# A transformer trunk on one core: a third chunk of the down projection by seven products, one weight sum by an adding transfer, and a buffer pair moved by some hundred bytes

## The chip, the cores and the metric

The kernel runs on one core of one Trainium2 chip. The metric is the device time of one execution in microseconds. The engines of a core are TensorE (PE, with its weight loads shown as PEld), VectorE (DVE), ScalarE (ACT), GpSimd (POOL) and SyncE (SP, which here only issues transfers). About 0.2%, 4.6 us, is what a measurement of this kernel can tell from no change.

## The reference

A two-layer encoder over 256 positions of width 2048, in float32:

```
h = x
h = h + mixer_a(rms_norm(h), ...)      # grouped-query attention, 16 heads
h = h + conv_ffn(rms_norm(h), ...)     # layer 0
h = h + mixer_b(rms_norm(h), ...)      # three dilated groups, 24 heads
h = h + conv_ffn(rms_norm(h), ...)     # layer 1
return rms_norm(h)

conv_ffn: u = conv3(h @ w_up) + b;  gate, val = split(u);  (silu(gate) * val) @ w_down
```

`w_up` is 2048 x 11264 and `w_down` is 5632 x 2048 in each layer. The change lies in the product with `w_down`.

## The kernel before

**Precision by splitting.** The kernel multiplies in a rounded form of float32 (type fp32r). Each operand is therefore cut into a high part (a rounding copy on ACT) and a low part (the rest, a subtraction on DVE), and a product takes three matmuls: high x high, low x high, high x low. For the weights, `split_raw` (line 116 on) makes `wh` (ACT, line 119) and `wl` (DVE, line 120) of each 128 x 1024 block. The activations, once split, are kept in `ah`/`al` tiles ("forms", 128 x 256 each).

**The buffers of the weights.** Six raw buffers `raw0` to `raw5` (`new_raw`) take blocks of 512 KB from memory, all issued from SP in program order. The ring `hl_ring` holds three pairs `wh`/`wl`. For the down projection a fourth pair, tag 9, is put in front of the ring (line 611) and taken out after it (line 657). The split of unit i can start when PE has used the pair of unit i-4.

**The FFN.** `ffn` (line 405) goes in two halves: `HALVES` gives 6 and then 5 pairs of 512-row chunks of the inner dimension. Each half first computes its part of the up projection (`feed_T`), the convolution (`up_post`) and the gate product (`glu` or `glu_forms`, the product on POOL), and then adds its part of the down projection to `h`. So the down projection's chunks are numbered 0 to 5 in a first half and 0 to 4 in a second.

**Seven products for eight.** In `project_pair` (line 214) the down projection works on two 512-column blocks of the output at once. A chunk is a 2 x 2 block problem: two blocks of 128 positions, 512 rows of weight as two 256-row blocks, two column blocks. A plain chunk takes 4 units of kind "c" with 12 matmuls each. A chunk listed in `SKG` is done by the Strassen-Winograd scheme: 7 units of kind "P" with 6 matmuls each. It needs sums of weight blocks (`prepare`, line 236: 11 += 12 for product 5, 12 += 22 for product 7, 22 += 11 for product 6, 21 += 22 for product 4; each is one DVE addition over 128 x 1024, line 241) and sums of activations (`glu_forms`). The four raw blocks 11, 12, 21, 22 of such a chunk are held until their last product, so two raw buffers are left for the plain units between. A first half runs two such passes (columns 0 and 1, then 2 and 3); a second half one, and the two other columns plainly (`project`).

**PSUM.** The pass uses all eight banks: M1, M5, M6, M7 for products that are combined afterwards, and C11, C21, C12, C22, to which plain units and the products 2, 3 and 4 add directly. `combine` (line 616) and `done` (line 555) bring them into `h` on DVE; they run a step at a time after units.

**The order of units** (lines 603 to 609): one plain unit, then each product followed by one plain unit, then the rest. `ORDER` gives the order of the products within a chunk. `late_at` marks the first unit of the last chunk, before which all pending work on the activations is drained.

**Priority.** Tile schedules instructions by program order; `tc.high_priority(offset=AHEAD)` lets a split or a weight sum go as if it had been written 45 instructions earlier. Each engine then works through its own list strictly in order.

**Where the tiles lie.** Pools are stacked in the order they are opened. In the program before, the forms of the outer pool (24 pairs), the inputs of the up projection and the three pairs `wh0` to `wl2` all start 448 bytes past a multiple of 1 KB in each partition. The FFN's own pool starts 704 bytes past one. In it lie, among others, the last six forms of a first half and the fourth pair:

| | FFN 0 | FFN 1 |
|---|---|---|
| `wh9`, bytes past a multiple of 1 KB | 768 | 768 |
| `wl9` | 896 | 768 |
| forms 24 to 29 | 896 | 768 |

In FFN 0 `bias_lines` (line 885) borrows the fourth pair's tiles during the up projection, to write position-bias lines for mixer B to memory.

Of the kernel before, what the change touches and what calls it, by code (L numbers as in the profile page):

```python
# [20 lines left out]
HALVES = ((0, 6), (6, 11))  # L21
SCALE = 128.0 ** -0.5
NRAW, NHL = 6, 3
SKG = ((0, 2), (0,))
ORDER = (1, 2, 5, 3, 7, 6, 4)
AHEAD = 45
NWARM = 11

# [2 lines left out]
def tile_encoder(ctx: ExitStack, tc: tile.TileContext, x, xT, w_a, w_ao, q_gain, k_gain, w_b, w_bo,  # L31
# [25 lines left out]
    def nm(s):  # L57
        uid[0] += 1
        return f"{s}_{uid[0]}"
# [154 lines left out]
    def project_pair(w, n0, n1, lhs, forms, units, late, early_done, n0_done):  # L214
        home = {1: "M1", 2: "C11", 3: "C12", 4: "C21", 5: "M5", 6: "M6", 7: "M7"}
        place = ("M1", "M5", "M6", "M7", "C11", "C21", "C12", "C22")
        b = bank_at[0]
        acc = {k: bank((4, 5, 6, 7, 2 - b, 3 - b, b, b + 1)[i], "acc") for i, k in enumerate(place)}

        def touched(u):  # L220
            return (home[u[2]],) if u[0] == "P" else (("C11", "C21"), ("C12", "C22"))[u[2] // 2]

        first, last = {}, {}
        for i, u in enumerate(units):
            for k in touched(u):
                first.setdefault(k, i)
                last[k] = i
        blocks = {}
        sums = {5: ("11", "12"), 7: ("12", "22"), 6: ("22", "11"), 4: ("21", "22")}

        def block(kg, b):
            if (kg, b) not in blocks:
                blocks[kg, b] = load_raw(w, (n0, n1)[int(b[1]) - 1], kg, int(b[0]) - 1)
            return blocks[kg, b]

        def prepare(u):
            kind, kg, p = u
            if kind == "P" and p in sums:
                dst, src = (block(kg, b) for b in sums[p])
                with tc.high_priority(offset=AHEAD):  # L240
                    nc.vector.tensor_tensor(dst, dst, src, ALU.add)
                if p == 6:
                    done_raw(blocks.pop((kg, "11")))
                elif p == 4:
                    done_raw(blocks.pop((kg, "22")))

        last_s = max(i for i, u in enumerate(units) if u[0] == "P")
        for i, (kind, kg, p) in enumerate(units):
            if i == late:
                drain()  # L250
            if kind == "c":
                r = load_raw(w, (n0, n1)[p // 2], kg, p % 2)
            else:
                b = {1: "11", 2: "21", 3: "22", 5: "11", 7: "12", 6: "22", 4: "21"}[p]
                r = block(kg, b)
            if i + 1 < len(units):
                prepare(units[i + 1])
            wh, wl = split_raw(r, kind == "c" or p in (7, 4))
            if kind == "P" and p in (7, 4):
                blocks.pop((kg, b))  # L260
            todo = []
            if kind == "c":
                for j in range(2):
                    for m, k in enumerate(touched((kind, kg, p))):
                        todo.append((k, *at(lhs[4 * kg + 2 * (p % 2) + j], m), j))
            else:
                xh, xl = forms[kg][p]
                for j in range(2):
                    todo.append((home[p], xh[:, j * P:(j + 1) * P], xl[:, j * P:(j + 1) * P], j))
            fresh = {k for k in acc if first[k] == i}  # L270
            for k, xh, xl, j in todo:
                nc.tensor.matmul(acc[k], xh, wh[:, j, :], start=k in fresh, stop=False)  # L272
                fresh.discard(k)
                nc.tensor.matmul(acc[k], xl, wh[:, j, :], start=False, stop=False)  # L274
            todo.sort(key=lambda t: (t[0], t[3]))
            for k, xh, xl, j in todo:
                nc.tensor.matmul(acc[k], xh, wl[:, j, :], start=False, stop=last[k] == i and j == 1)  # L277
            if i == last_s:
                early_done(acc)
            if i == last["C21"]:  # L280
                n0_done(acc)
            step()
        return acc
# [119 lines left out]
        more()  # L403

    def ffn(l, hT, ss_in, g_next, last, side=None):
        with tc.tile_pool(name=nm("fpool"), bufs=1) as fp:
            junk = junk_of(fp)
            rstd = finish_rstd(ss_in)
            part = small.tile([P, 2], F32, tag="part", name=nm("part"), bufs=1)
# [3 lines left out]
            rows = conv[l].rearrange("b o (r c) -> (b o r) c", c=P)  # L413
            nc.gpsimd.dma_start(cr[:, 0:2, :], rows[0:2 * P].rearrange("(a p) c -> p a c", p=P))
            nc.gpsimd.dma_start(cr[:NROW - 2 * P, 2, :], rows[2 * P:NROW])
            cw = fp.tile([P, NROW], F32, name=nm("cw"))

            def taps():
                t = ps_tile()
# [87 lines left out]
            kgs = list(range(4))  # L507
            for hf, (p0, p1) in enumerate(HALVES):
                slots, forms = {}, {}
                tags = iter([(hpool, k) for k in range(24)] + [(fp, k) for k in range(24, 30)])  # L510

                def new_form():
                    pool, k = next(tags)
# [2 lines left out]
                for p in range(p0, p1):  # L516
                    if p - p0 in SKG[hf]:
                        fm = forms[p - p0] = {f: new_form() for f in (1, 7, 2, 5, 4, 6, 3) + (0,) * hf}
                        if hf:
                            for kt in range(4):  # L520
                                slots[4 * (p - p0) + kt] = [
                                    tuple(t[:, kt % 2 * P:(kt % 2 + 1) * P] for t in fm[f])
                                    for f in ((1, 0), (2, 4))[kt // 2]]
                    else:
                        slots.update({4 * (p - p0) + j: new_form() for j in range(4)})
                    for hh in range(2):
                        cg = fp.tile([P, 2, NT], F32, tag="cg", name=nm("cg"), bufs=2)
                        cv = fp.tile([P, 2, NT], F32, tag="cv", name=nm("cv"), bufs=2)

                        def after(cg=cg, cv=cv, slots=slots, forms=forms, kg=p - p0, hh=hh):  # L530
                            if kg in forms:
                                return glu_forms(cg, cv, forms[kg], hh)
                            return glu(cg, cv, slots, 4 * kg + 2 * hh)

                        ga, va = new_acc(), new_acc()
                        parts = ([0, 1], [2], [3]) if p == 0 and hh == 0 else ([0, 1], [2, 3])
                        if len(parts) == 3:
                            for k, kk in enumerate(parts):
                                if k == 2:
                                    drain()  # L540
                                feed_T(ga, hT, w_up[l], p, hh, kk, k == 0, k == 2)
                                if k == 2:
                                    start(up_post(ga, p, hh, cg))
                                feed_T(va, hT, w_up[l], NPAIR + p, hh, kk, k == 0, k == 2)
                        else:
                            for k, kk in enumerate(parts):
                                feed_T(ga, hT, w_up[l], p, hh, kk, k == 0, k == 1)
                            start(up_post(ga, p, hh, cg))
                            for k, kk in enumerate(parts):
                                feed_T(va, hT, w_up[l], NPAIR + p, hh, kk, k == 0, k == 1)  # L550
                        start(up_post(va, NPAIR + p, hh, cv, after))
                    if p == 1 and side is not None:
                        spare.append(side(fp))

                def done(accs, n):
                    if hf == 1 and last:
# [45 lines left out]
                        fin.append(f)  # L602
                cs = [("c", k, i) for k in range(np_) if k not in SKG[hf] for i in range(4)]
                ps = [("P", k, p) for k in SKG[hf] for p in ORDER]
                per = max((len(cs) - 4) // len(ps), 1)
                units = [cs.pop(0)]
                for u in ps:
                    units += [u] + [cs.pop(0) for _ in range(per)]
                units += cs
                late_at = next(i for i, u in enumerate(units) if u[1] == np_ - 1)  # L610
                hl_ring.insert(0, (fp, 9))

                def hcol(m, n):
                    return h[:, m, n * 512:(n + 1) * 512]
# [38 lines left out]
                else:  # L653
                    seq = [k for k in range(np_)]
                    for n in (2, 3):
                        done(project(wd, n, slots, seq, last and hf == 1 and n == 3), n)
                hl_ring.remove((fp, 9))
            assert not spare
        return hTn, ss

# [221 lines left out]
    scr0 = dpool.tile([8, P, 512], F32, name="scr0")  # L882
    scr1 = dpool.tile([16, P, 256], F32, name="scr1")

    def bias_lines(lp):
        if True:
            oh = lp.tile([P, 1024], F32, tag="wh9", name="oh")
            nc.gpsimd.dma_start(oh, onehot)
            rb = lp.tile([P, 32], F32, name="rb")[:, :24]
            nc.gpsimd.memset(rb, 0.0)  # L890
            nc.gpsimd.memset(rb[32:33, :], -1e30)
            nc.gpsimd.dma_start(rb[:32, :], rel_bias)
            lh = lp.tile([P, 24, 32], F32, tag="wl9", name="lh")
            nc.vector.tensor_copy(lh, rb[:, :, None].to_broadcast([P, 24, 32]))
            for b in range(6):
                for _ in range(2):
# [2 lines left out]
                t = ps_tile()  # L899
                nc.tensor.matmul(t[:, :w], lh[:, 4 * b:4 * b + 4, :].rearrange("p a r -> p (a r)"),  # L900
                                 oh[:, c0:c0 + w], start=True, stop=True)
                ln = lp.tile([P, 512], F32, tag="ln", name=nm("ln"), bufs=2)
                nc.vector.tensor_copy(ln[:, :w], t[:, :w])
                dst = scr0[4 * b:4 * b + 4] if b < 2 else scr1[4 * (b - 2):4 * (b - 2) + 4]
                for i in range(4):
# [223 lines left out]
```

## Time and profile before

| | us |
|---|---|
| median of three runs | 2300.05 |
| lowest, highest run | 2299.35, 2300.75 |
| the profiled execution | 2300.93 |
| its span in the trace | 2299.2 |
| first half's down projection, FFN 0 | 543.6 to 670.2 |
| second half's, FFN 0 | 893.7 to 1001.9 |
| first half's, FFN 1 | 1831.4 to 1958.3 |
| second half's, FFN 1 | 2181.8 to 2290.2 |

The profile's page gives the busy time of each engine, the chain of waits that ended last (followed back from the last instruction), and the costliest groups of instructions: line, engine, operation, output <- inputs, shapes, count | busy us, mean ns of one | idle time of the engine before them and what ended it. A matmul's mean is from its start to its end; matmuls are pipelined. Rows of windows give, for a stretch of time, its length and each engine's busy time with the count of instructions, the granted clock, the DMA engines' busy share and GB/s. Rows of waits give who waited for whom: us in total, times, longest. Rows of transfers end with the median us from issue to landing.

### The profile page before, as it was taken

How to read it: one execution, taken by the hardware profiler on the slowest of the kernel's cores; microseconds unless marked ns; L12 is line 12 of the kernel's file. 1: busy time of each engine (PE TensorE's matmuls, PEld its weight loads, DVE VectorE, ACT ScalarE, POOL GpSimd, SP SyncE). 2: the span in 40 equal slices, each digit the busy share in tenths (PEclk: the TensorE clock that was granted, in tenths of full speed). 3: DMA queues.
4: the chain of work that ended last, by engine and by line, in shares of the span. 5: the costliest groups of instructions: out<-in, count | busy, mean ns of one | idle time of the engine just before them, and what ended most of it. 6: DMA issues, size and time to landing. Idle time of an engine off the chain costs nothing.

```text
span 2299.2 us, 31196 instructions
## 1 busy us (share of the span) xinstructions
PE 2281.6 (99%) x11581; PEld 1935.0 (84%) x11581; DVE 1732.5 (75%) x2483; ACT 1248.6 (54%) x1802; POOL 168.5 (7%) x130
## 2 busy tenths in 40 slices
PE   9999999999999999999999999999999999999998
PEld 7788788888888888888888888878888888888886
DVE  6877887777877778878876876576777788777774
ACT  6565565555545556445454454445555555565553
POOL 2210000010001010010000000000101000001110
PEclk9999999999999999999999999999999999999999
DMA  8444565765666555666655555566565566565663
GB/s 300 154 141 156 189 197 175 245 202 186 207 196 191 186 184 181 207 215 202 190 176 178 178 188 168 176 190 192 189 192 187 173 217 202 184 191 185 202 211 128
DMA packets 260313, 437.54 MB, mean 190 GB/s; under 512 B 13904, under 2 KB 196944, under 8 KB 260160
## 3 DMA queue, kind: packets, MB, share of 16 engines
q1 hardware_dynamic: 258080, 429.84, 58.3%
q0 software_dynamic: 1648, 5.15, 0.8%
q8 instruction: 90, 1.47, 0.3%
q14 instruction: 63, 0.52, 0.1%
q10 hardware_dynamic: 432, 0.56, 0.1%
HBM read 429.20 MB, written 6.29 MB: 189 GB/s over the span
## 4 chain that ended last, share of the span: by engine, by line
PE 93%; DVE 3%; DMA 1%; issue 1%; POOL 1%; ACT 0%; SPq 0%; POOLq 0%; DVEq 0%; ACTq 0%
PE acc L143 28%; PE acc L146 14%; PE acc L165 11%; PE acc L166 11%; PE acc L164 11%; PE acc L272 5%; PE acc L274 5%; PE acc L277 5%; DVE wl L120 1%; DVE tT L333 1%; PE ps L304 1%; DMA raw<-in_w_up_dram 1%; PE ps L308 1%; PE ps L307 1%; PE ps L306 0%
## 5 line engine op out<-in xcount | busy, mean ns | idle before, releaser
L119 ACT ACTIVATE wh<-raw 128x1024 fp32r<-128x1024 f32 x822 | 866.4, 1059 | 780.0 <-PE acc L166 276.5
L120 DVE TENSOR_TENSOR wl<-raw,wh 128x1024 fp32r<-128x1024 f32 x822 | 1007.7, 1231 | 369.5 <-ACT wh L119 356.8
L143 PE MATMUL acc<-xh,wh 128*128 128x512 f32 x2816 | 707.2, 393 | 0.8 <-ACT wh L119 0.8
L143 PEld LDWEIGHTS acc<-xh,wh 128*128 128x128 f32 x2816 | 507.0, 189 | 93.2 <-ACT wh L119 1.6
L146 PEld LDWEIGHTS acc<-xh,wl 128*128 128x128 f32 x2816 | 384.1, 190 | 27.5
L146 PE MATMUL acc<-xh,wl 128*128 128x256 f32 x2816 | 392.6, 282 | 0.0
L165 PE MATMUL acc<-wl,xh 128*128 128x512 f32 x768 | 300.2, 391 | 3.5 <-DVE wl L120 2.1
L164 PE MATMUL acc<-wh,xh 128*128 128x512 f32 x768 | 301.8, 394 | 0.0
L166 PE MATMUL acc<-wh,xh 128*128 128x512 f32 x768 | 299.5, 390 | 0.0
L272 PE MATMUL acc<-wh,ah 128*128 128x512 f32 x524 | 205.7, 393 | 0.0
L274 PE MATMUL acc<-wh,al 128*128 128x512 f32 x524 | 205.2, 392 | 0.0
L165 PE MATMUL acc<-wl,ah 128*128 128x512 f32 x480 | 188.0, 392 | 2.0 <-DVE wl L120 1.8
L164 PE MATMUL acc<-wh,ah 128*128 128x512 f32 x480 | 187.8, 391 | 0.0
L166 PE MATMUL acc<-wh,al 128*128 128x512 f32 x480 | 187.3, 390 | 0.0
L165 PEld LDWEIGHTS acc<-wl,xh 128*128 128x128 f32 x768 | 144.4, 188 | 34.0 <-DVE wl L120 4.6
L166 PEld LDWEIGHTS acc<-wh,xh 128*128 128x128 f32 x768 | 144.2, 188 | 30.0
L164 PEld LDWEIGHTS acc<-wh,xh 128*128 128x128 f32 x768 | 144.4, 188 | 27.8
L277 PE MATMUL acc<-wl,ah 128*128 128x512 f32 x524 | 146.9, 391 | 0.0
L466 POOL TENSOR_TENSOR cv<-cg,cv 128x512 f32<-128x512 f32 x32 | 73.2, 2288 | 651.6 <-DVE cv L458 591.2
L272 PEld LDWEIGHTS acc<-wh,ah 128*128 128x128 f32 x524 | 98.4, 188 | 22.0 <-ACT wh L119 0.2
L277 PEld LDWEIGHTS acc<-wl,ah 128*128 128x128 f32 x524 | 98.4, 188 | 21.8
L274 PEld LDWEIGHTS acc<-wh,al 128*128 128x128 f32 x524 | 98.4, 188 | 21.6
(175 smaller groups left out, 1838.9 us busy)
## 6 DMA issues: line engine op xcount, KB each, us to landing
raw<-in_w_up_dram SPq DMA_DIRECT2D x352, 512.0 KB, 5.0
raw<-in_w_down_dram SPq DMA_DIRECT2D x176, 512.0 KB, 4.4
raw<-in_w_b_dram SPq DMA_DIRECT2D x144, 512.0 KB, 4.2
raw<-in_w_bo_dram SPq DMA_DIRECT2D x48, 512.0 KB, 3.7
raw<-in_w_a_dram SPq DMA_DIRECT2D x40, 512.0 KB, 3.7
raw<-in_w_ao_dram SPq DMA_DIRECT2D x32, 512.0 KB, 3.6
raw<-in_w_a_dram SPq DMA_DIRECT2D x16, 256.0 KB, 6.5
h<-in_x_dram SPq DMA_DIRECT2D x4, 512.0 KB
```

Of the source, the lines that this page charges most:

```text
L119: nc.scalar.activation(wh, r, AF.Copy)
L120: nc.vector.tensor_tensor(wl, r, wh.bitcast(F32), ALU.subtract)
L143: nc.tensor.matmul(acc[j], wh[:, kt, j * P:(j + 1) * P], lhs[4 * kg + kt][2], start=first and i == 0 and kt == 0, stop=False)
L146: nc.tensor.matmul(acc[j][:, :NT], wl[:, kt, j * P:(j + 1) * P], lhs[4 * kg + kt][0], start=False, stop=end and kt == 3)
L164: nc.tensor.matmul(accs[m], xh, wh[:, j, :], start=st, stop=False)
L165: nc.tensor.matmul(accs[m], xh, wl[:, j, :], start=False, stop=False)
L166: nc.tensor.matmul(accs[m], xl, wh[:, j, :], start=False, stop=sp)
L272: nc.tensor.matmul(acc[k], xh, wh[:, j, :], start=k in fresh, stop=False)
L274: nc.tensor.matmul(acc[k], xl, wh[:, j, :], start=False, stop=False)
L277: nc.tensor.matmul(acc[k], xh, wl[:, j, :], start=False, stop=last[k] == i and j == 1)
L304: nc.tensor.matmul(o, lh[ls], rh[rs], start=start, stop=stop)
L466: nc.gpsimd.tensor_tensor(cv, cg, cv, ALU.mult)
```

## The change

1. `SKG` of a first half becomes (0, 2, 4): a third chunk by seven products. The units between products are spread anew: a first half has 21 products and 12 plain units, so that plain units follow the 3rd, 5th, 7th, ... 21st product. A second half keeps one plain unit after each product. The products' order becomes 1, 2, 3, 5, 7, 6, 4.
2. The sum 11 += 12 for product 5 is no longer a DVE addition. After block 11 has been split for product 1, a transfer issued from GpSimd adds block 12 to it (SBUF to SBUF, 512 KB).
3. A new pool `wpool` is opened before the FFN's pool. It holds the taps `cw`, padded from 1408 to 1792 bytes, the forms 24 to 32, and the fourth pair. All but `cw` then lie at 704 + 1792 = 2496 = 2 x 1024 + 448 bytes, or a multiple of 1 KB further.
4. To make room, `bias_lines` takes its two line buffers as the halves of one tile that shares the place of a transposition buffer.

```diff
-SKG = ((0, 2), (0,))
-ORDER = (1, 2, 5, 3, 7, 6, 4)
+SKG = ((0, 2, 4), (0,))
+ORDER = (1, 2, 3, 5, 7, 6, 4)
...
-            if kind == "P" and p in sums:
+            if kind == "P" and p in sums and p != 5:
...
+            if kind == "P" and p == 1:
+                with tc.high_priority(offset=AHEAD):
+                    nc.gpsimd.dma_start(r, block(kg, "12"), accum_op=ALU.add)
...
-        with tc.tile_pool(name=nm("fpool"), bufs=1) as fp:
+        with tc.tile_pool(name=nm("wpool"), bufs=1) as wp, tc.tile_pool(name=nm("fpool"), bufs=1) as fp:
+            cw = wp.tile([P, 448], F32, name=nm("cw"))[:, :NROW]
...
-            cw = fp.tile([P, NROW], F32, name=nm("cw"))
...
-                tags = iter([(hpool, k) for k in range(24)] + [(fp, k) for k in range(24, 30)])
+                tags = iter([(hpool, k) for k in range(24)] + [(wp, k) for k in range(24, 33)])
...
-                per = max((len(cs) - 4) // len(ps), 1)
+                between = min(len(cs) - 2 - 6 * hf, len(ps))
                 units = [cs.pop(0)]
-                for u in ps:
-                    units += [u] + [cs.pop(0) for _ in range(per)]
+                for i, u in enumerate(ps):
+                    units.append(u)
+                    if (i + 1) * between // len(ps) > i * between // len(ps):
+                        units.append(cs.pop(0))
...
-                hl_ring.insert(0, (fp, 9))
+                hl_ring.insert(0, (wp, 9))
...
-    def bias_lines(lp):
+    def bias_lines(wp, lp):
...
+            lnt = lp.tile([P, 2, 512], F32, tag="tT", name="lnt")
...
-                ln = lp.tile([P, 512], F32, tag="ln", name=nm("ln"), bufs=2)
+                ln = lnt[:, b % 2]
```

More of the change, by code (lines that the diff above doesn't have):

```diff
@@ L552, in ffn @@
                     if p == 1 and side is not None:
-                        spare.append(side(fp))
+                        spare.append(side(wp, fp))
                 def done(accs, n):
@@ L656, in ffn @@
                         done(project(wd, n, slots, seq, last and hf == 1 and n == 3), n)
-                hl_ring.remove((fp, 9))
+                hl_ring.remove((wp, 9))
             assert not spare
@@ L883, in tile_encoder @@
     scr1 = dpool.tile([16, P, 256], F32, name="scr1")
-    def bias_lines(lp):
+    def bias_lines(wp, lp):
         if True:
-            oh = lp.tile([P, 1024], F32, tag="wh9", name="oh")
+            oh = wp.tile([P, 1024], F32, tag="wh9", name="oh")
             nc.gpsimd.dma_start(oh, onehot)
@@ L892, in bias_lines @@
             nc.gpsimd.dma_start(rb[:32, :], rel_bias)
-            lh = lp.tile([P, 24, 32], F32, tag="wl9", name="lh")
+            lh = wp.tile([P, 24, 32], F32, tag="wl9", name="lh")
+            lnt = lp.tile([P, 2, 512], F32, tag="tT", name="lnt")
             nc.vector.tensor_copy(lh, rb[:, :, None].to_broadcast([P, 24, 32]))
```

## The prediction

> **What bounds the kernel now.** I read the page's busy shares first, then the chain of waits, then the costliest groups.
>
> ```profile
> PE 2281.6 (99%) x11581; PEld 1935.0 (84%) x11581; DVE 1732.5 (75%) x2483; ACT 1248.6 (54%) x1802; POOL 168.5 (7%) x130
> ...
> PE 93%; DVE 3%; DMA 1%; issue 1%; POOL 1%; ACT 0%; SPq 0%; POOLq 0%; DVEq 0%; ACTq 0%
> ...
> L272 PE MATMUL acc<-wh,ah 128*128 128x512 f32 x524 | 205.7, 393 | 0.0
> ```
>
> PE is busy 99% and is 93% of the chain that ended last, so a matmul taken away shortens the end, as long as the other engines still feed PE. The trap is its price. The 393 ns of L272 is the time from a matmul's start to its end, and matmuls overlap. What one costs is the distance between starts, which the windows give: stretches of PE alone, with the count of weight loads (one for each matmul).
>
> ```profile
> 210.06:239.98 29.92, 29.92 (x133) 24.77 (x132) 26.20 (x42) 16.00 (x24) 0.00 (x0) 1.00 0.55 176
> ...
> 543.60:670.22 126.62, 103.69 (x553) 1.00 0.62 199
> 893.66:1001.90 108.24, 89.01 (x475) 1.00 0.60 195
> 1831.38:1958.32 126.94, 103.66 (x553) 1.00 0.62 199
> 2181.79:2290.20 108.41, 88.75 (x474) 1.00 0.49 160
> ```
>
> The first row lies in mixer A's output projection, which has no fourth pair: 132 matmuls in 29.92 us, 226.7 ns each. The other four rows (columns: length, PEld busy and count, clock, DMA share, GB/s) are the down projections, first and second half of FFN 0, then of FFN 1. By the code a first half has 552 matmuls (two passes of 14 units of 6 and 16 of 12) and a second half 474 (234 in the pair, 240 after it); one load at an edge is a neighbour's. At 226.7 ns these are 125.12 and 107.44 us. The stretches are longer by 1.50, 0.80, 1.82 and 0.97 us, 5.1 together. The starts of units say where, in the timeline of PE (start, length of one, line):
>
> ```profile
> 547.81 0.39 PE L272 MATMUL acc<-wh,ah 128*128 128x512 f32 x1
> ...
> 550.53 0.39 PE L272 MATMUL acc<-wh,ah 128*128 128x512 f32 x1
> ...
> 551.89 0.40 PE L272 MATMUL acc<-wh,ah 128*128 128x512 f32 x1
> ...
> 554.67 0.40 PE L272 MATMUL acc<-wh,ah 128*128 128x512 f32 x1
> ...
> 556.05 0.39 PE L272 MATMUL acc<-wh,ah 128*128 128x512 f32 x1
> ```
>
> These are the first matmuls of units 2 to 6. A plain unit of 12 takes 2.72 us, a product of 6 takes 1.36: 226.7 ns again. Unit 4, every fourth, is fed by the fourth pair, and takes 2.78; the next takes 1.38. Nobody waits there. By the program's addresses the three pairs of the ring and the 24 forms of the outer pool all lie 448 bytes past a multiple of 1 KB; the fourth pair lies at 768 and 896 (FFN 0) or 768 and 768 (FFN 1), and so do the last six forms.
>
> **Part one: a third chunk by seven products.** In one pass over two column blocks a plain chunk is 4 units of 12 matmuls, a chunk by products 7 of 6: 42 for 48. One chunk, two passes, two layers: 24 matmuls fewer, at 226.7 ns **5.4 us** less on the path.
>
> The page "TensorE: Matmul & The Clock Gate" of the Trainium skill, section "Back-to-back issue gap", gives about 131 ns for a sustained matmul of N=512. By that the part would be worth an estimated 3.1 us; the 132 matmuls above disagree, so I stay with 226.7.
>
> The price is more splits (ACT copy, DVE subtraction) for less PE time. DVE's timeline and its window over the second pass show how near it is:
>
> ```profile
> 586.59 1.22 DVE L120 TENSOR_TENSOR wl<-raw,wh 128x1024 fp32r<-128x1024 f32 x1
> 587.73 1.22 DVE L241 TENSOR_TENSOR raw<-raw,raw 128x1024 f32<-128x1024 f32 x1
> 588.86 3.49 DVE L120 TENSOR_TENSOR wl<-raw,wh 128x1024 fp32r<-128x1024 f32 x3
> ...
> 607.00:670.20 63.20, 63.20 (x277) 51.79 (x276) 51.38 (x51) 31.21 (x31) 0.00 (x0) 1.00 0.63 200
> ...
> L387 DVE TENSOR_TENSOR h<-acc,h 128x512 f32<-128x512 f32 x7 | 4.7, 684 | 0.7 <-PE acc L277 0.7
> ...
> ACT wh L119 <- PE acc L274: 44.1, 42, 3.1
> ...
> DVE raw L241 <- DMA raw<-in_w_down_dram: 8.0, 5, 3.2
> ```
>
> Back to back, splits and sums start 1.14 us apart. A pass before needs 30 splits and 8 sums, 43.3 us, and 12 operations of L387's kind (combination and residual) at 0.68, 8.2: 51.5, as the window's 51.38 shows, of 63.2. After: 33 splits and 9 sums (a tenth to twelfth go to the transfer), 47.9 + 8.2 = 56 us, of 21 x 1.36 + 12 x 2.72 = 61.2. So 92%, still under PE; with every sum on DVE it would be 59.5. Locally, P P c needs 3 splits and about 1 sum, 4.6 us of 5.4, and the tightest stretch, P5 P7 c P6 P4 c, 6 splits and 3 sums, 10.3 of 10.9: no debt, but no lead won either. ACT (33 copies of 1.06, 35 us) is far away. The lead is what hides all this. In the waits between 543 and 680 us ACT stands 44.1 us for PE to release a buffer: splits run at the ring's full depth. I cost the denser units at 0, hidden by that lead. Without it each of the 8 tight stretches (chunks 0 and 4, two passes, two layers) would make PE wait for about one DVE operation more: 8 x 1.14 = 9 us, the upper bound.
>
> Smaller things. The product P3 now makes C12 needed three units into a pass instead of four longer ones: in the second pass 5.44 us after its start. The two L387 additions that must clear C12 and C22 were done 3 us after the start (606.98):
>
> ```profile
> 608.73 1.28 DVE L387 TENSOR_TENSOR h<-acc,h 128x512 f32<-128x512 f32 x2
> ...
> L290 DVE TENSOR_TENSOR al<-st,ah 128x256 fp32r<-128x256 f32 x24 | 9.6, 419 | 0.0
> L289 ACT ACTIVATE ah<-st 128x256 fp32r<-128x256 f32 x24 | 9.5, 406 | 0.0
> ...
> 407.00:541.00 134.00, 133.24 (x761) 116.89 (x760) 102.85 (x154) 79.28 (x119) 13.18 (x6) 1.00 0.69 221
> ```
>
> That leaves 2.4 us: 0, at most 1 per layer if DVE has no lead then. And the third chunk's forms cost, once a layer, 3 more ACT copies (0.41), 3 more subtractions and 4 sums on DVE (0.42 each, 2.9 us), in the up stage, where DVE works 102.85 of 134: 0. The bias lines now alternate between halves of one tile; their six steps spread over 63 us, so 0.
>
> **Part two: the fourth pair's position.** The new pool starts where the old one did, 704 past a multiple of 1 KB, and its first tile is padded to 1792 bytes, so pair and late forms come to 448 like the others. If position is the cause, all of the 5.1 us go, except 0.1 that is a wait for a copy: **5.0 us**. Bounds: 0 (no effect) and 5.1.
>
> **Part three: the first sum by a transfer.** Off DVE, one sum per chunk and pass (14 in all). On POOL, 14 issues, each waiting for P1's subtraction and block 12. Behind it on POOL stands at most the last gate product, used only by the last chunk. On ACT and DVE P5's copy waits for the landing, and *every* later split stands behind that. No row shows an adding transfer; the nearest are POOL's plain ones:
>
> ```profile
> oh<-in_onehot_dram POOLq DMA_DIRECT2D x1, 512.0 KB, 5.1
> rb<-in_rel_bias_dram POOLq DMA_DIRECT2D x1, 3.0 KB, 4.6
> fin<-in_final_norm_dram POOLq DMA_DIRECT2D x4, 256.0 KB, 6.3
> ...
> DMA to landing us min/median/max: 6.1/6.3/7.1
> ...
> q1 hardware_dynamic: 258080, 429.84, 58.3%
> ```
>
> Lower bound 5.1 us, the plain 512 KB. The adding one must also read its destination: 429.84 MB in 58.3% of 2299.2 us is 321 GB/s, so one more pass over 0.524 MB is 1.6 us: 6.7. Upper bound: the slowest landing of POOL's queue (fin's, 7.1) and two passes more, 10.4. I take 6.7, since only the pass is new to the 512 KB row.
>
> The page "Collectives: The Full Stack", section "Part 3: Why 7× under link rate — side-by-side accounting", says that an add in a DMA costs no arithmetic but needs two source reads, which halves the rate. That speaks against the transfer as the row does; by a full doubling at the row's rate an estimate is the same 6.7.
>
> How long it may take: in chunks 0 and 2 P5 starts 6.8 us after P1 (three products and a plain unit between, P1 included), and its copy takes 1.1. With no lead at P1 the transfer may take 5.7; with the ring full (three units and a third, 5.9, less the split's 2.4) 3.5 more, 9.2. In chunk 4, with two plain units between, 8.4 to 11.9; in second halves still more. At 6.7 it costs something only where the lead is under 1.0 us. **I allow +1.0 us** in all. The load of weights grows to 206 GB/s and the transfers add 26 to 51, a share of 0.72 to 0.80 where it is 0.62 now: landings stay hidden as DVE's 8.0 us of waits for them are now.
>
> **The sum.** The profiled execution took 2300.93 us (span 2299.2, 1.7 around it), 0.9 above the median 2300.05. 2300.93 - 5.4 - 5.0 + 1.0 = 2291.5, against the median **2290.6**.
>
> **Rivals.**
> - *Only the count pays.* Position is not the cause and the slow units stay: 2300.05 - 5.4 + 1 = 2295.6. Against it: units of the three aligned pairs are at 226.7 to the nanosecond, and no wait stands there.
> - *DVE becomes the bound in the dense stretches.* 92% on average with no lead regained between P5 and P4; the 9 us of the upper bound above: 2300.05 - 10.4 + 9 = 2298.7. Against it: 5.2 us of slack per pass.
> - *The transfer lands late* (the other side). Place: the copy for P5, with all splits behind it. At the upper 10.4 us and the middle of 5.7 and 9.2, it is 2.9 us late in the 8 near chunks, and late by nearly nothing in the 4 far ones; ACT and DVE have to refill the lead in a stretch that gives none. 8 x 2.9 = 23 us, so 2300.05 - 10.4 + 23 = 2313. It becomes slower than before once the loss is over 10.4 us, that is 1.3 per near chunk: a transfer over 8.8 us. For it: all 16 engines are shared with loads at a share of 0.62, and the adding form is unknown. Against it: 512 KB on the same queue took 5.1.
>
> **How the numbers follow.** Forecast with 0 to 3 us of stalls (2288.5 to 2293): 0.60. Count alone: 0.08. DVE-bound or slightly late, 2293 to 2301: 0.12. Late transfer: 0.20. The range goes from 2288.5 (everything hidden, less the runs' spread) to 2303, leaving out most of the late transfer; the likeliest case's own range is 2288.5 to 2293. About 0.2% (4.6 us) can be told from no change: faster (under 2295.4) takes the forecast, half of the count alone and half of the third case, 0.70; the same 0.11; slower 0.19.
>
> **What would show it.** Matmuls of line 272 fall from 524 to 516. Every unit of the pairs takes 2.72 or 1.36 us, and the first halves 122.4 us each (540 matmuls). The transfers' landing is under 8 us and PE waits for ACT's copy less than 1 us in all. I am wrong if the fourth unit still takes 2.78, or if PE's idle before L272 is several us released by ACT, which itself waited for the transfer on P5.

## The result, and the profile after

| | us | ratio to before, 95% interval |
|---|---|---|
| before, median of the runs beside it | 2300.23 | |
| after, median of four runs (2315.5 to 2321.4) | 2317.3 | 1.0077 [1.0060, 1.0095] |
| predicted | 2290.6 (2288.5 to 2303) | |
| the profiled execution of after, its span | 2318.56, 2316.7 | |

The change makes the kernel 17 us slower. The page of the kernel after (busy shares, the chain of waits, two groups, one row of transfers):

```profile
PE 2284.1 (99%) x11557; PEld 1934.2 (83%) x11557; DVE 1747.4 (75%) x2511; ACT 1261.1 (54%) x1820; POOL 180.3 (8%) x144
...
PE 86%; DVE 6%; DMA 4%; issue 2%; ACT 1%; POOL 1%; SPq 0%; POOLq 0%; DVEq 0%; ACTq 0%
...
L275 PE MATMUL acc<-wh,ah 128*128 128x512 f32 x516 | 204.3, 396 | 1.9 <-ACT wh L119 1.9
...
L280 PE MATMUL acc<-wl,ah 128*128 128x512 f32 x516 | 149.6, 397 | 15.0 <-DVE wl L120 14.9
...
raw<-raw POOLq DMA_DIRECT2D x14, 512.0 KB, 6.8
```

The 24 matmuls are gone (516 for 524 on each of three lines), yet PE is busy longer and has fallen from 93% to 86% of the chain; DVE and DMA have taken the difference. PE now stands 14.9 us ahead of line 280, the matmuls with the *low* part of the weights, which DVE makes. The wait that the prediction feared, before the high part (line 275, released by ACT), is only 1.9. The transfer lands in 6.8 us in the median; 6.7 was estimated. Its fastest and slowest landings stand in the view of the tile:

```profile
DMA to landing us min/median/max: 4.6/6.8/8.1
```

Where it happens, by windows over the four down projections (length, PE and PEld busy with counts, DVE, ACT, POOL, granted clock, DMA share, GB/s):

```profile
542.72:680.10 137.38, 128.22 (x542) 102.94 (x541) 111.33 (x113) 70.59 (x74) 6.45 (x6) 0.98 0.66 202
903.54:1011.80 108.26, 108.26 (x480) 89.64 (x479) 91.72 (x130) 54.55 (x74) 3.24 (x1) 1.00 0.60 195
1840.39:1974.62 134.23, 128.11 (x542) 102.96 (x541) 111.30 (x113) 70.72 (x74) 6.41 (x6) 0.97 0.67 206
2198.06:2306.50 108.44, 106.88 (x470) 87.54 (x469) 66.50 (x70) 47.64 (x59) 13.24 (x7) 1.00 0.51 164
```

A first half should take 540 x 0.2267 = 122.4 us. It takes 137.4 and 134.2: 15.0 and 11.8 us lost. By the starts of its units, the pair pass of FFN 1's second half loses 2.5 more, that of FFN 0's nothing. So some 29 us are lost against 10.4 gained; the span is 17.5 us longer, so that the 1.4 us between lie outside the down projections. The waits say to what:

```profile
DVE raw L241 <- DMA raw<-raw: 40.2, 12, 5.4
...
PEld acc L280 <- DVE wl L120: 22.6, 19, 3.4
...
PE acc L280 <- DVE wl L120: 14.9, 13, 3.0
...
ACT wh L119 <- DMA raw<-raw: 10.4, 7, 2.0
```

DVE's *sums* (line 241) stand 40.2 us for the adding transfer, 12 times, up to 5.4. ACT's copies, where the prediction put the wait, stand 10.4. PE's longest stall, in chunk 4 of FFN 0's first pass, in the chain of waits (start, length, what):

```profile
583.68 8.10 DMA raw<-raw
...
591.88 1.06 ACT wh L119
592.95 1.23 DVE wl L120
594.18 0.04 issue
594.22 0.80 PE acc L280 x2
```

and the same moments in the timelines of DVE, ACT and PE:

```profile
591.80 1.23 DVE L241 TENSOR_TENSOR raw<-raw,raw 128x1024 f32<-128x1024 f32 x1 [4.32 <-DMA raw<-raw]
592.95 2.36 DVE L120 TENSOR_TENSOR wl<-raw,wh 128x1024 fp32r<-128x1024 f32 x2
...
587.06 1.06 ACT L119 ACTIVATE wh<-raw 128x1024 fp32r<-128x1024 f32 x1 [0.83 <-DMA raw<-in_w_down_dram]
...
590.18 0.39 PE L275 MATMUL acc<-wh,ah 128*128 128x512 f32 x1
```

Which blocks these are, the program's instruction list for DVE tells (in its order: line, output <- inputs):

```
L241 raw_5653<-raw_5653,raw_5692    12 += 22, for product 7; waits for the transfer
L120 wl_5695<-raw_5692,wh_5694      low part for product 3
L120 wl_5707<-raw_5704,wh_5706      low part of the plain unit
L241 raw_5692<-raw_5692,raw_5647    22 += 11, for product 6
L120 wl_5724<-raw_5647,wh_5723      low part for product 5
```

The sum 12 += 22 overwrites block 12, which the transfer reads. So it waits for the landing, and in DVE's list it stands *ahead of product 3's subtraction*. Product 3's copy was done at 588.12 (587.06 + 1.06), its subtraction could have run then, and it ran at 592.95. PE, which began product 3 at 590.18 and needs the low part at its fifth matmul, stood until 594.22. Product 5's copy, at 591.88, was in time: by the units' lengths PE would have come to it at 590.18 + 1.36 + 2.72 = 594.26.

In FFN 1's second half the same sum waits 4.98 us, against 2.34 in FFN 0's, which loses nothing:

```profile
2201.86 1.23 DVE L241 TENSOR_TENSOR raw<-raw,raw 128x1024 f32<-128x1024 f32 x1 [4.98 <-DMA raw<-raw]
```

Behind it in DVE's list stand, beside splits, the last steps of the convolution. They come later there, and with them the gate product and the copy of its form, ahead of a weight copy on ACT that PE then waits for. That this is the whole 2.5 us is read from one trace and was not tested.

### The profile page after: what moved, and what is told of

Read it like the earlier page. It is cut to its first block, busy times and chain, and to the rows that moved or that the text cites. A ratio compares the mean times of both kernels' runs of the same rounds, so it can differ in the third digit from the quotient of the medians.

```text
span 2316.7 us, 31266 instructions
## 1 busy us (share of the span) xinstructions
PE 2284.1 (99%) x11557; PEld 1934.2 (83%) x11557; DVE 1747.4 (75%) x2511; ACT 1261.1 (54%) x1820; POOL 180.3 (8%) x144
## 4 chain that ended last, share of the span: by engine, by line
PE 86%; DVE 6%; DMA 4%; issue 2%; ACT 1%; POOL 1%; SPq 0%; POOLq 0%; DVEq 0%; ACTq 0%
PE acc L143 27%; PE acc L146 14%; PE acc L165 11%; PE acc L166 11%; PE acc L164 11%; PE acc L280 3%; PE acc L275 3%; PE acc L277 3%; DVE wl L120 3%; DMA raw<-raw 3%; DVE tT L336 1%; DMA raw<-in_w_down_dram 1%; ACT wh L119 1%; PE ps L307 1%; DMA raw<-in_w_up_dram 1%
## 5 line engine op out<-in xcount | busy, mean ns | idle before, releaser
L119 ACT ACTIVATE wh<-raw 128x1024 fp32r<-128x1024 f32 x834 | 877.6, 1058 | 783.8 <-PE acc L166 277.1
L280 PE MATMUL acc<-wl,ah 128*128 128x512 f32 x516 | 149.6, 397 | 15.0 <-DVE wl L120 14.9
L280 PEld LDWEIGHTS acc<-wl,ah 128*128 128x128 f32 x516 | 96.5, 190 | 41.9 <-DVE wl L120 22.6
L165 PEld LDWEIGHTS acc<-wl,ah 128*128 128x128 f32 x480 | 90.1, 188 | 23.9 <-DVE wl L120 5.7
```

What stands on the lines that cost most here:

```text
L119: nc.scalar.activation(wh, r, AF.Copy)
L165: nc.tensor.matmul(accs[m], xh, wl[:, j, :], start=False, stop=False)
```

## The experiments

Chunks, products and blocks are named as above; a *chunk pass* is one chunk by products in one pass over two column blocks (twelve in the first halves, two in the second). What a unit loses is its length on PE less 226.7 ns a matmul. Medians in us; before took 2300.6 to 2301.1 beside these runs.

**1. The position alone** (two chunks, old order, all sums on DVE; only the new pool).

> The kernel before with only the position changed: new pool, fourth pair and late forms 448 bytes past a multiple of 1 KB; two chunks by seven products, all sums on DVE. If position is the cause of the slow fourth unit, every unit takes 2.72 or 1.36 us, the four down-projection stretches lose their excess of 5.1 us, and the time is about 2300.2 - 5.0 = 2295.2. If position is no cause, it stays at 2300.

Measured: 2296.1, ratio 0.9981 [0.9972, 0.9991]. The windows of its two first halves:

```profile
543.38:668.52 125.14, 125.14 (x554) 103.61 (x553) 102.84 (x106) 64.75 (x68) 3.25 (x1) 1.00 0.62 202
...
1828.92:1954.07 125.15, 125.15 (x555) 103.61 (x553) 103.23 (x106) 64.70 (x68) 3.25 (x1) 1.00 0.62 202
```

These were 126.62 and 126.94, and 552 x 0.2267 = 125.14: no unit of them is slow any more. The position is the cause of the slow fourth unit. The run moves the pair and the late forms together, so it does not tell which of them counts, nor which addresses would be bad.

**2. The sum back on DVE.**

```diff
-            if kind == "P" and p in sums and p != 5:
+            if kind == "P" and p in sums:
...
-            if kind == "P" and p == 1:
-                with tc.high_priority(offset=AHEAD):
-                    nc.gpsimd.dma_start(r, block(kg, "12"), accum_op=ALU.add)
```

> The changed kernel with the sum 11 += 12 given back to DVE; third chunk, order and position stay. Theory A (the transfer and the waits for it are the whole loss): the first halves fall to the floor of 122.4 us each, and the time to 2300.2 - 5.4 - 5.0 = 2290, at most 2293. Theory B (DVE has too little room in the dense stretches, 59.5 of 61.2 us a pass): PE still waits for DVE's low parts, about 1.14 us in each of 8 tight stretches, some 2299.

Measured: 2297.7, 0.9985 [0.9976, 0.9994]. The first halves lose 3.9 and 4.8 us, in products 2 and 3 of chunk 4 and, in the second passes, products 2, 6 and 4 of chunk 0. That looks like theory B, and would have been taken for it without run 5.

**3 and 4. The sum 12 += 22 moved back in DVE's list.** Run 3 puts it behind product 3's subtraction:

```diff
-                    nc.vector.tensor_tensor(dst, dst, src, ALU.add)
+                    if p == 7:
+                        with tc.issue_after(p3_sub[kg]):
+                            nc.vector.tensor_tensor(dst, dst, src, ALU.add)
+                    else:
+                        nc.vector.tensor_tensor(dst, dst, src, ALU.add)
```

> The changed kernel, but the sum 12 += 22 may not stand ahead of the subtraction for product 3 in DVE's list; everything else stays. Theory A1 (product 3's low part waits behind a sum that waits for the landing): the first instruction that the landing can hold up is now one product later, 1.36 us, in the 8 near chunk passes where PE stalled by up to 3.4 us. At least half of the 29 us of stalls goes: 2300 to 2307. Theory A2 (the copy for product 5 waits, as the prediction had it) or loads that come late because of the transfer: nothing changes, 2315 to 2319.

Run 4 puts it behind the last subtraction written before it (`last_sub[-1]` in place of `p3_sub[kg]`).

> The changed kernel, but the sum 12 += 22 stands behind the subtraction of the last unit split before it: in chunks 0 and 4 behind that of the plain unit between products 3 and 5, in chunk 2 behind that of product 5. Theory A1: in chunks 0 and 4 the landing has 4.1 us more than in the changed kernel, in chunk 2 1.36 us more, so of the stalls a little of chunk 2 is left: 2292 to 2302. Theory A2 or late loads: nothing changes, 2315 to 2319.

Measured: 2302.05, 1.0007 [0.9997, 1.0016], and 2302.4, 1.0006 [0.9996, 1.0015]. One place in a list gives back 15 us, so A1 holds. But moving the sum further brings nothing more (2292 to 2302 was expected), and 12 us against run 5 stay. The windows of run 4's first halves, with 5.3 and 8.8 us lost:

```profile
542.49:670.16 127.67, 125.13 (x542) 100.61 (x541) 110.39 (x110) 70.13 (x74) 6.45 (x6) 1.00 0.69 214
1830.50:1961.73 131.23, 126.45 (x542) 99.92 (x541) 110.34 (x111) 69.90 (x74) 6.41 (x6) 1.00 0.67 209
```

Over half of it (7.9 of 14.1) lies in products 6 and 4, whose sums come last in the row 12 += 22, 22 += 11, 21 += 22. In run 4 no sum waits for the landing any more; ACT's copy for product 5 does:

```profile
ACT wh L121 <- DMA raw<-raw: 8.0, 5, 2.6
```

That is the place where the prediction had put the wait.

**5. Sum on DVE, block 12 fetched at product 1.** The transfer needs block 12 at product 1; run 2 fetched it only for product 5. This adds to run 2:

```diff
+            if kind == "P" and p == 1:
+                block(kg, "12")
```

> The sum 11 += 12 on DVE as in the run with all sums there (2297.7), but block 12 is fetched at product 1, as the transfer needs it, so that one more of the six raw buffers is held for two units. Theory F (the early fetch makes the other loads late, and that is what the transfer costs beyond its wait): 2301 to 2304. If not: within 1.5 us of 2297.7.

Measured: 2290.2, 0.9952 [0.9936, 0.9969]. Theory F falls, and the opposite is true: the early fetch *saves* 7.5 us. Its first halves, and its longest wait of a sum for a load, beside that of run 2:

```profile
546.13:668.56 122.43, 122.43 (x543) 101.36 (x541) 115.74 (x116) 70.67 (x74) 3.25 (x1) 1.00 0.62 205
1828.98:1951.41 122.43, 122.43 (x543) 101.36 (x541) 115.64 (x116) 70.59 (x74) 3.25 (x1) 1.00 0.63 204
...
DVE raw L241 <- DMA raw<-in_w_down_dram: 1.8, 5, 0.6
```

```profile
DVE raw L241 <- DMA raw<-in_w_down_dram: 22.0, 14, 3.9
```

Both first halves stand at their floor, with every sum on DVE: it is busy 115.7 of 122.4 us (95%) and PE waits for nothing. So DVE is not the bound there, even at 95%. What run 2 showed was a sum waiting for a late block with splits behind it, the same pattern as the transfer's with another cause.

**6. Without the sum.**

> The changed kernel without the sum 11 += 12 altogether: no transfer, no addition on DVE; product 5 works on block 11 alone, so this part of the result is left out. It is the floor for any way of moving that sum off DVE. Theory D (what is left beside product 3's wait is debt from the landing): with nothing to land, no unit stalls, first halves 122.4 to 123 us each, 2290 to 2291. Theory E (products 6 and 4 are short of DVE time of their own): PE still loses about 0.9 us at product 4 in most of the 12 chunk passes of the first halves, and the time stays at 2294 or more.

Measured: 2293.1, 0.9967 [0.9955, 0.9979]: 3 us *more* than with the sum on DVE and the early fetch. It fits neither theory. Here block 12 is fetched only for product 7, and the sums of line 241 wait for loads:

```profile
DVE raw L241 <- DMA raw<-in_w_down_dram: 29.0, 10, 4.8
```

So it is no floor. It agrees with run 5 in that a late block costs time.

**7 and 8. The sum on GpSimd,** with block 12 fetched for product 5, then at product 1.

```diff
+                    (nc.gpsimd if p == 5 else nc.vector).tensor_tensor(dst, dst, src, ALU.add)
```

> The changed kernel, but the sum 11 += 12 is an addition on GpSimd. By its 2.29 us for 128x512 it should take about 4.6 us for 128x1024, against 6.8 us to the landing of the transfer, and it moves no bytes through the DMA engines. If only the time to the sum and DVE's load count: 2290 to 2296, better than all sums on DVE (2297.7). If DVE runs slower while GpSimd adds (subtractions of over 1.2 us next to it): 2298 or more.

> The sum 11 += 12 on GpSimd as in the run at 2313.3, and block 12 fetched at product 1. GpSimd's addition took 2.49 us, but it waited 216 us in all for loads of blocks. If the late fetch made that run slow: 2289 to 2293, like DVE's sum with the early fetch (2290.2). If GpSimd itself is the cause: 2300 or more.

Measured: 2313.3, 1.0056 [1.0040, 1.0072], and 2293.1, 0.9966 [0.9953, 0.9979]. GpSimd's waits in the first:

```profile
POOL raw L241 <- DMA raw<-in_w_down_dram: 215.8, 13, 21.3
DVE raw L241 <- POOL raw L241: 51.0, 12, 6.9
```

The addition itself takes 2.49 us, not the 4.6 expected. The late fetch costs 20 us here, because DVE's next sum waits for GpSimd's; with the fetch moved, nearly all of it goes.

**9. An idle transfer, two chunks.** Run 1, and an adding transfer of block 12 into a scratch tile:

```diff
+                    nc.gpsimd.dma_start(scratch[0], block(kg, "12"), accum_op=ALU.add)
```

> The run with the position alone (2296.1; two chunks, all sums on DVE) plus an adding transfer of block 12 into a tile that nobody reads, ten in all, so that only GpSimd and the DMA engines have the work and block 12's buffer is read by one more party. Theory G (the transfers' bytes crowd the loads): each takes about 2.8 us of all 16 engines, loads come late, 2300 or more. If bytes do not matter: 2295 to 2297.5.

Measured: 2297.5, 0.9986 [0.9977, 0.9995]. The first halves take what they take in run 1, to 0.02 us. With a plain unit after each product the bytes cost nothing there.

**10. A needed transfer, two chunks.** As run 4, with the chunks and plain units of before.

> Two chunks by seven products with a plain unit after each product, as before the change, new position, order 1, 2, 3, 5, and the sum 11 += 12 by the transfer, 12 += 22 behind the subtraction of the last unit before it. Product 5 starts 3 x 1.36 + 3 x 2.72 = 12.2 us after product 1, so a landing of 7 us is never late. Theory H: no unit stalls, the same time as the position alone: 2295 to 2297.5. Theory J: 10 transfers cost something of the 12 us that 14 cost in three chunks, 2300 or more.

Measured: 2296.0, 0.9978 [0.9969, 0.9987]: the time of run 1, and no unit is late. With 12 us from product 1 to product 5 the change's own transfer is free.

**11. Half the bytes.** As run 4, with 256 KB by the transfer and the other half on DVE.

> The kernel with the sum 12 += 22 behind the plain unit's subtraction (2302.4), but the transfer adds only the first half of block 12 (256 KB), and DVE the second half (0.6 us). Block 12 is fetched at product 1 in both. Theory H (what is left of the loss comes from the landing being late): the transfer lands about 1.5 us sooner, so most of the 12 us between 2302.4 and 2290.2 goes: 2291 to 2297. Theory J (the loss has another cause in the issue from GpSimd or in the crowding of the DMA engines by whatever bytes): 2299 or more.

Measured: 2297.9, 0.9984 [0.9975, 0.9994]; the transfer lands in 4.8 us.

```profile
raw<-raw POOLq DMA_DIRECT2D x14, 256.0 KB, 4.8
```

Landing 2.1 us sooner than run 4's 6.9 gives back 4.6 of the 12 us: less than H expected (2291 to 2297), more than J.

**12. An idle transfer of 320 KB out of block 12, three chunks,** on run 5.

> The best kernel so far (sum on DVE, block 12 fetched at product 1, 2290.2) plus, in each of the 14 chunk passes, an adding transfer of 5/8 of block 12 (320 KB) into a tile that nobody reads, issued where the changed kernel issues its transfer. Theory H (only the waiting for the landing costs): 2289 to 2292. Theory J (the transfers' bytes or issues cost by themselves in the dense stretches): 5/8 of the 12 us, 2297 or so.

Measured: 2304.6, 1.0016 [1.0007, 1.0025]. That seems to speak for J, but the run was not what it was meant to be:

```profile
DVE raw L243 <- DMA scratch<-raw: 21.9, 10, 3.6
```

Nobody reads the scratch tile, yet DVE's sum 12 += 22 waits for the transfer, since it overwrites the transfer's *source*.

**13. The same out of block 21,** which only the sum for product 4 overwrites.

```diff
-                    nc.gpsimd.dma_start(scratch[0], block(kg, "12")[:, :, :320], accum_op=ALU.add)
+                    block(kg, "12")
+                    nc.gpsimd.dma_start(scratch[0], block(kg, "21")[:, :, :320], accum_op=ALU.add)
```

> As the run with the idle transfer of 320 KB in each of the 14 chunk passes, but out of block 21, which is overwritten only by the sum for product 4, some 10 us after product 1, instead of block 12, which the sum for product 7 overwrites. Sum on DVE, block 12 fetched at product 1. Theory H (only waits for a landing cost): the 14 us between 2304.6 and 2290.2 go: 2289 to 2293. Theory J (bytes or issues cost in the dense stretches): the time stays over 2297.

Measured: 2289.7, 0.9952 [0.9938, 0.9965], the time of run 5. The same bytes from the same queue cost 15 us where a sum waits for them and nothing where none does: H holds, J falls.

**14. Run 5 again.**

> The best kernel again, with more runs: 2289 to 2292, and under the kernel before in every run.

Measured: 2289.3 (2289.1 to 2290.4), 0.9951 [0.9939, 0.9964]. It beats the kernel before by 11 us and the changed one by 28.

**15. One step further:** `SKG = ((0, 2, 4), (0, 2))` on run 5.

> The best kernel with a second chunk by seven products in each second half as well: 6 matmuls fewer in each of the two layers' pair passes. If DVE still has room there: 2290.2 - 12 x 0.2267 = 2287.5. If the second half's pass, now with 14 products and 6 plain units between and behind them, is short of DVE or of loads: 2290 or more.

Measured: 2289.3, 0.9954 [0.9940, 0.9967]: no gain. Each second half's pass has 228 matmuls for 234 but takes 53.1 us as before, where 228 x 0.2267 = 51.7; the weight loads wait there for low parts (PEld at line 279 for line 120, 3.5 us in all), each time at products 5, 6 and 4 of the new chunk.

## Why the prediction was wrong, step by step

- **The count** (-5.4) was right. The 516 matmuls of each line are there, and run 5's first halves are 122.43 us where 122.4 was forecast. This again speaks for 226.7 ns a matmul, and against the 131 ns that the Trainium skill gives ("TensorE: Matmul & The Clock Gate", section "Back-to-back issue gap").
- **The position** (-5.0) was right: run 1 shows -4.5 in the medians, and the slow units are gone.
- **Denser units at 0** was right in itself: in run 5, with every sum on DVE, nothing stalls in the first halves at 95%. The forecast for that case, 59.5 us of DVE a pass, was a little high (57.9). The rival "DVE becomes the bound" is refuted by run 5.
- **The transfer's own time** was right in the median: 6.7 forecast, 6.8 measured. By their bytes alone the transfers delay nothing: run 9 (512 KB, two chunks) and run 13 (320 KB, three chunks) cost no time. In the kernel after, ACT's copies do wait 50.5 us for loads of `w_down`, against 24.3 before; in run 13 it is 32.3, in run 5 29.8. So this seems to come with the waits for the landing, since a late sum frees its raw buffers late, and not with the bytes. The full 512 KB in the dense order without a wait were not tried.
- **The step that failed is "How long it may take".** It counted from product 1 to product 5's copy: 5.7 us with no lead to 9.2 with a full ring in chunks 0 and 2, and 8.4 to 11.9 in chunk 4. It asked who *reads* the sum, and not who *overwrites* the source, nor where that one stands. With 12 += 22 ahead of product 3's subtraction, the landing was due at the fifth matmul of product 3, less one split and one sum on DVE. In chunks 2 and 4 that is 2 x 1.36 + 2.72 + 4 x 0.2267 - 1.22 - 1.14 = 4.0 us after the start of product 1. The lead was smaller than the 3.5 us allowed, too: by the trace these transfers were issued 0.6 to 2.4 us before that start. So they had 4.5 to 6.4 us, and took 6.3 to 8.1. PE stood 1.0 to 3.1 us inside product 3 in seven of these eight chunk passes; in the eighth the transfer had 6.4 and took 6.3. The stall shown above is one of them: issued at 583.68, 1.06 us before product 1's start (590.18 - 5.44), it had 5.1 us; it took 8.10, and PE went on 3.1 us after its 591.09. These seven waits are 13.2 us, and slow matmuls behind four of them (last section) 6.4 more, where the sum allowed +1.0 for everything.
- **Chunk 0 shows that it is the place in the list and the lead that decide.** It has no plain unit before product 3, so the same count leaves only 1.3 us. Yet product 3 is never late there. In the second passes the sum stands behind product 3's subtraction in DVE's list. In the first passes the transfer was issued 6.4 us before product 1 started (at 545.47), and the sum was done in time:

```profile
539.05 0.94 POOL L263 DMA_DIRECT2D raw<-raw  x1 [10.33 <-DMA raw<-in_w_down_dram]
...
543.68 1.23 DVE L241 TENSOR_TENSOR raw<-raw,raw 128x1024 f32<-128x1024 f32 x1 [2.14 <-DMA raw<-raw]
```

- **"Every later split stands behind that"** was wrong in the same way: an *earlier* split stood behind it. The hoist (`high_priority`) does not keep a sum behind the splits written before it.
- **The rival "lands late"**, with a chance of 0.20 and 2313, had the right sign. That its time is near is luck: it priced a landing of 10.4 us, and in the kernel after none took over 8.1. Its threshold of 8.8 us was passed by no transfer either; the kernel became slower all the same, since the wait was in another place. Run 4 has the wait where the rival put it: there, with landings of 6.9 us in the median and 9.7 at most, the loss about eats up the gain.
- **The sum.** 10.4 gained as forecast, and 29 lost in place of 1.0. Of these 15 go with the one place in DVE's list (run 3). The rest goes where nothing waits for a transfer (run 13) or the landing has time (run 10).

What stays open is the division of that rest. In run 4, 9.0 of the 14.1 us lie in chunk 2, where the sums for products 7, 6 and 4 stand behind product 5's subtraction, and with it behind its copy, which waits for the landing. But 3.0 lie in chunk 0 of the two first passes, and nothing waits for the landing there. The sum for product 4 stands in that chunk behind a low part of a form (line 299), which waits 1.63 us for its copy on ACT, and this for GpSimd's product. In run 5 it stands ahead of the like one:

```profile
555.75 0.76 DVE L299 TENSOR_TENSOR al<-cv,ah 128x256 fp32r<-128x256 f32 x2 [1.63 <-ACT ah L298]
556.42 1.22 DVE L247 TENSOR_TENSOR raw<-raw,raw 128x1024 f32<-128x1024 f32 x1
```

```profile
552.33 1.22 DVE L241 TENSOR_TENSOR raw<-raw,raw 128x1024 f32<-128x1024 f32 x1
...
560.17 0.76 DVE L292 TENSOR_TENSOR al<-cv,ah 128x256 fp32r<-128x256 f32 x2 [1.63 <-ACT ah L291]
```

So the order that comes with the transfer probably costs something too; no run moves this one sum alone.

## What to carry to other kernels

When work moves to a transfer, list everyone who must wait for it: the readers of its result and the writers of its source and destination. Then look, in the in-order list of each engine, at what stands behind the first of these; the deadline is there, and not where the result is used. Two stalls that look alike (a sum that holds up the splits behind it) can have different causes, so a late load is to be ruled out before an engine is called full.

## What the hardware showed unexpectedly

After some stalls PE's matmuls start 427 ns apart instead of 227, for about 3.5 us. After the stall shown above (the kernel after; start and length on PE):

```profile
590.86 0.39 PE L277 MATMUL acc<-wh,al 128*128 128x512 f32 x1
594.22 0.80 PE L280 MATMUL acc<-wl,ah 128*128 128x512 f32 x2 [2.97 <-DVE wl L120]
594.82 0.63 PE L275 MATMUL acc<-wh,ah 128*128 128x512 f32 x1
595.25 0.63 PE L277 MATMUL acc<-wh,al 128*128 128x512 f32 x1
...
597.81 0.57 PE L277 MATMUL acc<-wh,al 128*128 128x512 f32 x1
598.21 1.08 PE L280 MATMUL acc<-wl,ah 128*128 128x512 f32 x4
599.13 0.39 PE L275 MATMUL acc<-wh,ah 128*128 128x512 f32 x1
```

Eight matmuls at 0.2 us extra each make the stall 1.6 us dearer. The kernel after has two such stretches in each first half, and the granted clock of these halves reads 0.98 and 0.97, where run 5 has none and reads 1.00. A shorter stall can do it and a longer one not: the first two rows below are the kernel after, the others run 12.

```profile
1870.88 0.84 PE L280 MATMUL acc<-wl,ah 128*128 128x512 f32 x2 [1.80 <-DVE wl L120]
1871.52 0.63 PE L275 MATMUL acc<-wh,ah 128*128 128x512 f32 x1
```

```profile
654.54 0.73 PE L282 MATMUL acc<-wl,ah 128*128 128x512 f32 x2 [2.32 <-DVE wl L120]
655.11 0.40 PE L277 MATMUL acc<-wh,ah 128*128 128x512 f32 x1
```

An idle of 1.80 us is followed by slow matmuls (0.63), one of 2.32 by fast ones (0.40). The Trainium skill ("TensorE: Matmul & The Clock Gate", section "Part 1: The HAM clock gate (the "warmup" mystery)") gives N / 1.2 GHz, 426.7 ns, as the pace of a cold array at N = 512, and a window of about 3.4 us that runs freely. The pace and the length of the slow stretch agree with that; that an idle time much shorter than a window can be enough is what these rows add.
